# Turning round the column order of a decoder step's main products: moving columns read and sums written from last to first

## The chip, the cores and the metric

The kernel runs on one core of one Trainium2 chip. The metric is the device time of one execution in microseconds, lower being better; the runs shown are three executions of the kernel as it was. The profile is one execution taken by the hardware profiler. It names the engines PE (TensorE, matrix products), PEld (TensorE's loading of weights), DVE (VectorE), ACT (ScalarE), POOL (GpSimd) and SP (SyncE, which issues DMAs). L488 is line 488 of the kernel.

## The reference

The program computes one layer of a decoder for a prompt of 256 tokens and for 8 samples of 4 tokens each, which share all weights. Cut to what matters here:

```
h = rms_norm(x, g_mix)
proj = h @ w_in                       # conv, q, k, v, memory q, three gates
y_conv = silu(layer_norm(conv(...))) @ w_conv_out
y_sb   = stick_breaking(...) @ w_sb_out
y_mem  = memory_attend(...) @ w_mem_out
merged = g0 * y_conv + g1 * y_sb + g2 * y_mem
x = x + merged @ w_o
x = x + square(relu(rms_norm(x, g_mlp) @ w_up)) @ w_down
```

D_MODEL is 2048, the inner width of the last pair is 8192, all values are fp32. Besides the two outputs the program returns new keys, values, convolution states and memory keys and values.

## The kernel before

All activations stand transposed: a tile has 128 features on the partitions and the T = 288 tokens (256 of the prompt, then 32 of the samples) as columns. A weight matrix is cut into blocks of 128 x 128. Eight such blocks under each other, 512 KB, make a slab of `wall`, and the program walks through 504 slabs in one fixed order: w_kv, w_in, the branch projections between the gates, w_o, then four rounds of w_up and w_down.

Each slab is loaded by a DMA from SP into a buffer of pool `wr` (4 buffers). ScalarE rounds it into a high part of type fp32r in pool `wh` (L305), and VectorE takes the difference as a low part in pool `wl` (L316); each has 4 buffers. Activations are split in the same way, into `a.h` and `a.l`. One product then needs three matmuls for each block of 128 x 128: high weights with the high activations, high weights with the low ones, low weights with the high ones. `products` makes this list for a slab, 24 matmuls, and gives it to `chunk` in parts of six. `chunk` issues the matmuls (L488): the weights `w` are the stationary operand, 128 columns, and the activations `a` are the moving operand, 288 columns. All matmuls of one output tile add into the same bank of PSUM, `ps`, whose first 288 columns are used. `main_tile` takes two slabs (16 blocks of features) for one output tile of 128 features and then hands the bank to an evacuation on VectorE. `conv_products` calls `chunk` as well, for the first four tiles. The products of the prompt's memory tokens, in `mem_products` (L541, 512 moving columns), the attention's small products and the column sums in `total` (L443 and L444) do not go through `chunk`.

Where the operands lie in their tiles is fixed by a few constants:

```
APART = 320
AHEAD, HOME = 4, 36
PAD = 64
SHIFT = 5
```

Activations of pool `a` start at column 4 of a tile of 320 columns (`Acts`). The hidden activations of the last part live in `homes`, three to a buffer of pool `k4` from column 36 on, 320 columns apart, and one to a buffer of pool `s` from column 36 on. The weight slabs start at column 5 of their tile, apart from the first sixteen. The tiles of pool `t`, which `total` reads, and `ones_r` start at column 0.

The order of instructions on each engine is fixed by a planner (`Order`) when the program is built: jobs ask for an engine, a duration and buffers, and the one that can start first is taken, ties by rank. TensorE's instructions thus run in one planned order, and waits between engines are semaphores.

Of the kernel before, what the change touches and what calls it, by code (L numbers as in the profile page):

```python
# [183 lines left out]
def tile_decoder_step(ctx: ExitStack, tc: tile.TileContext, xT, memT, wall, cvec, kmat, ptab,  # L184
                      kpool, vpool, mkc, mvc, hist,
                      yT, oK, oV, oCp, oCs, oMK, oMV):
    nc = tc.nc
# [297 lines left out]

    def chunk(ps, todo, first, last):
        for i, (w, a) in enumerate(todo):
            nc.tensor.matmul(ps, w, a, start=(first and i == 0), stop=(last and i == len(todo) - 1))  # L488

    slab_no = [0]  # L490
    FULL = [k * P for k in range(8)]
# [2 lines left out]
    def products(ps, uses, acts, first=True, last=True, n=T):  # L494

        s = slab_no[0] - 1
        sl = slabs[s]
        high = [(sl.h, c, a, x) for c, a in zip(uses, acts) for x in (0, 1)]
        low = [(sl.l, c, a, 0) for c, a in zip(uses, acts)]
        todo = high + low  # L500
        for i in range(0, len(todo), STEP):
            part = todo[i:i + STEP]
            yield pe(len(part) * MM, *sl.split, *{a.flag for _, _, a, _ in part})
            if i == 0 and first:
                start_slab(s)
            chunk(ps, [(w[:, c:c + P], a.l if x else a.h) for w, c, a, x in part],
                  first and i == 0, last and i + STEP >= len(todo))
# [42 lines left out]
    def conv_products(evacs):  # L550
# [8 lines left out]
        for k2, o in turns:  # L559
            s = s0 + k2  # L560
            sl = slabs[s]
            if len(ps) <= o:
                yield pe(0.0, pm=1)
                ps.append(bank("pm")[:, :T])
            todo = []
            for i in range(2):
                w = slice(i * 512 + o * P, i * 512 + (o + 1) * P)
                todo += [(sl.h, w, "h", 2 * k2 + i), (sl.h, w, "l", 2 * k2 + i)]
            for i in range(2):
                todo.append((sl.l, slice(i * 512 + o * P, i * 512 + (o + 1) * P), "h", 2 * k2 + i))  # L570
            yield pe(6 * MM, *sl.split, hx_in[2 * k2], hx_in[2 * k2 + 1])
            if o == 0:
                start_slab(s)
            chunk(ps[o], [(w[:, c], getattr(hx[k], x)) for w, c, x, k in todo], k2 == 0, k2 == KT // 2 - 1)
            if k2 == KT // 2 - 1:
                add(evacs[o](ps[o]), 1.0 + 0.01 * o)
            if o == 3:
                give("w")
# [1042 lines left out]
```

## Time and profile before

| | |
|---|---|
| median of three runs | 1634.39 us |
| lowest, highest | 1634.28, 1634.63 us |
| span of the profiled execution, first to last instruction | 1632.5 us |
| matmuls | 12786, as many weight loads |
| matmuls of L488 | 11712 |
| HBM read | 297.05 MB, 186 GB/s over the span |
| granted TensorE clock | 1.000 |

The page gives busy time for each engine, the chain of work that ended last, and groups of instructions by line, with the busy time, the mean length of one, and the idle time before them. The length of a matmul is from its start to the modelled end of its results, so two matmuls that follow each other overlap; the distance between their starts is shorter than the length of one. That distance is read from a piece of the chain, or from a window, by dividing its length by the number of matmuls in it. The names on the two sides of the arrow are pools: `pm<-k,wl` is a matmul that writes a bank of pool pm and reads activations in a buffer of pool k4 and low weights.

### The profile page before, as it was taken

To read this page: it belongs to the slowest core of one execution; us is meant where nothing else is said; L and a number is where in the kernel's file an instruction comes from. 1 tells how busy PE (TensorE), PEld (TensorE's weight loads), DVE (VectorE), ACT (ScalarE), POOL (GpSimd) and SP (SyncE) were. 2 spreads that over 40 slices of the span, in tenths; PEclk is the share of its full clock that TensorE was granted. 3 is DMA by queue.
4 is the path that set the end of the run, shared out by engine and by line. 5 is a ranking of instruction groups with operands and counts; after the bars stand their busy time and mean duration, and the time that the engine had idled before them with its cause. 6 is when DMAs were issued, how large, how long until landed. Compare 5 with 4: busy or idle time off the path is not lost.

```text
span 1632.5 us, 30962 instructions
## 1 busy us (share of the span) xinstructions
PE 1627.7 (100%) x12786; PEld 1610.3 (99%) x12786; DVE 992.1 (61%) x1471; ACT 739.3 (45%) x1070; POOL 139.1 (9%) x104
## 2 busy tenths in 40 slices
PE   9999999999999999999999999999999999999999
PEld 7999999999999999999999999999999999999999
DVE  8889888877677655565555544455445554455443
ACT  8746766644444534444443333333333333333332
POOL 0020000000000000001222200121001210022100
PEclk9999999999999999999999999999999999999999
DMA  9787465777755555546655555555555555555563
GB/s 339 217 186 251 153 209 189 248 257 252 254 166 169 163 179 167 174 153 212 191 176 168 169 168 168 169 169 174 165 173 170 168 170 169 168 168 168 180 194 99
DMA packets 107103, 305.39 MB, mean 187 GB/s; under 512 B 19922, under 2 KB 29522, under 8 KB 106962
## 3 DMA queue, kind: packets, MB, share of 16 engines
q1 hardware_dynamic: 106818, 303.39, 58.2%
q8 instruction: 100, 1.64, 0.4%
q14 instruction: 41, 0.34, 0.1%
q10 hardware_dynamic: 144, 0.02, 0.0%
HBM read 297.05 MB, written 6.32 MB: 186 GB/s over the span
## 4 chain that ended last, share of the span: by engine, by line
PE 99%; DMA 0%; SPq 0%; ACT 0%; DVE 0%; issue 0%
PE pm L488 93%; PE pm L541 3%; PE pa L488 1%; PE pl L1017 1%; PE pl L1190 0%; PE pa L854 0%; PE pa L855 0%; PE pa L853 0%; DMA wr<-in_wall 0%; PE pl L1033 0%; PE pa L827 0%; PE pa L1144 0%; PE pa L908 0%; PE pa L1141 0%; PE pa L1143 0%; PE pa L1107 0%
## 5 line engine op out<-in xcount | busy, mean ns | idle before, releaser
L305 ACT CAST wh<-wr 128x1024 fp32r<-128x1024 f32 (+1 forms) x520 | 530.3, 1022 | 648.1 <-PE pm L488 597.0
L488 PE MATMUL pm<-a,wh 128*128 128x288 f32 x5184 | 739.1, 293 | 0.0
L316 DVE TENSOR_TENSOR wl<-wr,wh 128x1024 fp32r<-128x1024 f32 (+1 forms) x520 | 617.2, 1190 | 195.2 <-ACT wh L305 190.5
L488 PEld LDWEIGHTS pm<-a,wh 128*128 128x128 f32 x5184 | 696.7, 188 | 1.3 <-issue 1.2
L488 PE MATMUL pm<-a,wl 128*128 128x288 f32 x2592 | 397.0, 292 | 0.0
L488 PEld LDWEIGHTS pm<-a,wl 128*128 128x128 f32 x2592 | 358.4, 188 | 0.0
L488 PE MATMUL pm<-k,wh 128*128 128x288 f32 x2160 | 306.7, 292 | 0.0
L488 PEld LDWEIGHTS pm<-k,wh 128*128 128x128 f32 x2160 | 290.2, 188 | 0.0
L488 PE MATMUL pm<-k,wl 128*128 128x288 f32 x1120 | 171.6, 292 | 0.0
L488 PEld LDWEIGHTS pm<-k,wl 128*128 128x128 f32 x1120 | 155.1, 188 | 0.0
L1346 POOL TENSOR_TENSOR t<-t 128x288 f32<-128x288 f32 x64 | 96.7, 1511 | 599.5 <-DVE t L1343 599.5
L1360 DVE TENSOR_TENSOR a<-a,pm 128x288 f32<-128x288 f32 x64 | 29.0, 454 | 122.4 <-PE pm L488 122.4
L1343 DVE SCALAR_TENSOR_TENSOR t<-pm,rx 128x288 f32<-128x288 f32 x64 | 29.2, 457 | 90.4 <-PE pm L488 90.4
L1349 ACT CAST k<-t 128x288 fp32r<-128x288 f32 x56 | 24.1, 433 | 115.6 <-POOL t L1346 115.6
L1262 DVE TENSOR_TENSOR t<-pm,rx 128x288 f32<-128x288 f32 x48 | 22.0, 458 | 71.5 <-PE pm L488 71.5
L488 PE MATMUL pm<-s,wh 128*128 128x288 f32 x400 | 65.1, 292 | 0.0
L719 DVE SCALAR_TENSOR_TENSOR a<-a,cv,a 128x256 f32<-128x256 f32 x120 | 57.5, 480 | 1.4
L1332 POOL TENSOR_TENSOR t<-t,t 128x288 f32<-128x288 f32 x15 | 21.6, 1441 | 419.3 <-ACT t L1329 419.3
L488 PEld LDWEIGHTS pm<-s,wh 128*128 128x128 f32 x400 | 56.6, 188 | 0.0
L1351 DVE TENSOR_TENSOR k<-t,k 128x288 fp32r<-128x288 f32 x52 | 23.8, 458 | 51.1 <-ACT k L1349 51.1
L541 PE MATMUL pm<-wh,a 128*128 128x512 f32 x128 | 34.6, 391 | 0.2 <-ACT wh L305 0.2
L488 PE MATMUL pm<-s,wl 128*128 128x288 f32 x160 | 33.8, 292 | 0.0
(212 smaller groups left out, 784.4 us busy)
## 6 DMA issues: line engine op xcount, KB each, us to landing
wr<-in_wall SPq DMA_DIRECT2D x488, 512.0 KB, 3.6
wr<-in_wall SPq DMA_DIRECT2D x32, 256.0 KB, 4.8
k<-in_kpool SPq DMA_DIRECT2D x32, 256.0 KB, 5.9
k<-in_vpool SPq DMA_DIRECT2D x32, 256.0 KB, 5.8
k<-in_mkc SPq DMA_DIRECT2D x8, 512.0 KB, 10.2
k<-in_mvc SPq DMA_DIRECT2D x8, 512.0 KB, 6.5
t<-in_xT SPq DMA_DIRECT2D x16, 144.0 KB, 3.7
out_yT<-a SPq DMA_DIRECT2D x16, 144.0 KB, 1.9
```

The source lines that it names most:

```text
L305: nc.scalar.copy(sl.h[:, c], sl.raw[:, c])
L316: nc.vector.tensor_sub(sl.l[:, c], sl.raw[:, c], sl.h[:, c].bitcast(F32))
L488: nc.tensor.matmul(ps, w, a, start=(first and i == 0), stop=(last and i == len(todo) - 1))
L541: nc.tensor.matmul(ps[m], y[:, m * P:(m + 1) * P], z[:, w], start=(k == 0 and j < 2), stop=(k == KT - 1 and j in (4, 5)))
L719: nc.vector.scalar_tensor_tensor(c[:, :NP], up[:, k:k + NP], w, c[:, :NP], op0=ALU.mult, op1=ALU.add)
L1262: nc.vector.tensor_mul(g, ps, rx)
L1332: nc.gpsimd.tensor_add(sq_sum[0], sq_sum[0], res[0])
L1343: nc.vector.scalar_tensor_tensor(r, ps, 0.0, r2, op0=ALU.max, op1=ALU.mult)
L1346: nc.gpsimd.tensor_mul(r, r, r)
L1349: nc.scalar.copy(a.h, r)
L1351: nc.vector.tensor_sub(a.l, r, a.h.bitcast(F32))
L1360: nc.vector.tensor_add(x1[j], x1[j], ps)
```

## The change

One line of `chunk` is changed. The moving operand is given to the matmul as a view with its columns in reverse, and so is the output. Column 287 of the activations is read first and its sums are written to column 287 of the bank first; column 0 is last. Since both views are turned round, every sum lands where it did before. The stationary operand, the start and stop flags, the order of matmuls, all buffers, starts of tiles, engines and waits are as they were. Every engine has the same instructions in the same order.

```
 def chunk(ps, todo, first, last):
     for i, (w, a) in enumerate(todo):
-        nc.tensor.matmul(ps, w, a, start=(first and i == 0), stop=(last and i == len(todo) - 1))
+        nc.tensor.matmul(ps[:, ::-1], w, a[:, ::-1], start=(first and i == 0), stop=(last and i == len(todo) - 1))
```

## The prediction

> **What bounds the kernel now.** I read the page's table of busy time first, then the chain of waits, then what the TensorE itself waited for, and last how evenly it runs.
>
> ```profile
> span 1632.5 us, 30962 instructions
> PE 1627.7 (100%) x12786; PEld 1610.3 (99%) x12786; DVE 992.1 (61%) x1471; ACT 739.3 (45%) x1070; POOL 139.1 (9%) x104
> PEclk9999999999999999999999999999999999999999
> PE 99%; DMA 0%; SPq 0%; ACT 0%; DVE 0%; issue 0%
> PE pm L488 93%; PE pm L541 3%; PE pa L488 1%; PE pl L1017 1%; PE pl L1190 0%; PE pa L854 0%; PE pa L855 0%; PE pa L853 0%; DMA wr<-in_wall 0%; PE pl L1033 0%; PE pa L827 0%; PE pa L1144 0%; PE pa L908 0%; PE pa L1141 0%; PE pa L1143 0%; PE pa L1107 0%
> ```
>
> The chain that ends last is TensorE for 99% of the span, and line 488, the one line that the change edits, is 94% of it. Busy time alone would not prove this, since the ends of matmuls are modelled. The list of waits does: this is all that TensorE waited for other engines, and beside it the longest wait on the other side.
>
> ```profile
> PE pa L1409 <- POOL eps L234: 1.3, 1, 1.3
> PE pm L541 <- ACT wh L305: 0.2, 1, 0.2
> ACT wh L305 <- PE pm L488: 597.0, 341, 4.1
> ```
>
> TensorE lost 1.5 us to others in 1632.5 us. ScalarE, which casts the weights, waited 597.0 us for TensorE to free buffers. So the weights are always there early, and the time of this program is the number of matmuls times the pace at which TensorE takes them.
>
> That pace comes from the chain in order of time (start, length, how many), and does not depend on what else runs, as two windows show (PE, PEld, DVE, ACT and POOL busy, then the granted clock, the DMA share and GB/s).
>
> ```profile
> 17.79 31.28 PE pm L541 x138
> 541.70 297.18 PE pm L488 x2286
> 839.15 790.15 PE pm L488 x6078
> 600.00:700.00 100.00, 100.00 (x771) 100.00 (x770) 58.02 (x82) 42.75 (x55) 0.00 (x0) 1.00 0.54 168
> 1000.00:1200.00 200.00, 200.00 (x1541) 200.00 (x1540) 97.95 (x113) 72.56 (x80) 24.27 (x16) 1.00 0.54 169
> ```
>
> 790.15 us / 6078 = 130.0 ns from one matmul of 288 columns to the next, and 297.18 / 2286 = 130.0 ns too, over stretches that read their moving columns from three kinds of buffers. The windows give 129.7 ns with DVE 58% busy and 129.8 ns with DVE 49% busy. A pace this even is made inside each matmul, not by traffic of the other engines. The matmuls of 512 columns at line 541 take 31.28 / 138 = 226.7 ns. Two points give a line: (226.7 - 130.0) / (512 - 288) = 0.432 ns for a column, so 288 columns are 124.3 ns and 5.7 ns is left over for each matmul.
>
> **The change part by part.** It removes and adds no instruction and moves none; each engine has the same rows in the same order. The same sums land in the same columns of the same bank, because the moving columns and the output columns are both turned round. So VectorE reads what it read before and no wait changes. Only two address streams inside the matmul of line 488 run downwards: the moving read, from its tile's last column, and the accumulating write.
>
> How many matmuls that is, by group:
>
> ```profile
> L488 PE MATMUL pm<-a,wh 128*128 128x288 f32 x5184 | 739.1, 293 | 0.0
> L488 PE MATMUL pm<-a,wl 128*128 128x288 f32 x2592 | 397.0, 292 | 0.0
> L488 PE MATMUL pm<-k,wh 128*128 128x288 f32 x2160 | 306.7, 292 | 0.0
> L488 PE MATMUL pm<-k,wl 128*128 128x288 f32 x1120 | 171.6, 292 | 0.0
> L488 PE MATMUL pm<-s,wh 128*128 128x288 f32 x400 | 65.1, 292 | 0.0
> L488 PE MATMUL pm<-s,wl 128*128 128x288 f32 x160 | 33.8, 292 | 0.0
> L488 PE MATMUL pa<-a,wh 128*128 128x288 f32 x64 | 11.1, 295 | 0.0
> L488 PE MATMUL pa<-a,wl 128*128 128x288 f32 x32 | 6.8, 292 | 0.0
> ```
>
> Together 11,712. At 130.0 ns they are 1522.6 us of the 1632.5 us; the other 110 us (the 512-column products, the attention's small matmuls, start and tail) are not edited. So one nanosecond per matmul is worth 11.7 us, or 0.72%, and nothing hides it: TensorE is the chain. The profiled span lies 1.9 us under the median of the runs, 1634.39 us; I carry that as it is. The whole question is one number: what the 130.0 ns become.
>
> No row of this trace shows a matmul that reads or writes downwards. The only reversed operands are those of VectorE's scan at line 1204, another engine and an operation of its own. So I bound the cost from both sides.
>
> Below: the least that the fit leaves is the 124.3 ns of the columns, if turning the streams removed the whole 5.7 ns at the seam between two matmuls. 11,712 x 5.7 = 67 us, so 1567 us. The faster side cannot be excluded, since two streams are read side by side: the timeline has the weight load for the next matmul start with the present one.
>
> ```profile
> 1627.82 0.42 PE L488 MATMUL pm<-s,wh 128*128 128x288 f32 x2
> 1627.83 0.19 PEld L488 LDWEIGHTS pm<-s,wh 128*128 128x128 f32 x1
> ```
>
> The two starts are 0.01 us apart and the load takes 0.19 us, longer than the 0.130 us to the next matmul. Where a moving stream and a weight stream meet depends on where each starts and which way it runs.
>
> Above, in small: the matmuls of the same form (288 columns, fp32r, accumulated into a bank) whose tiles start at other columns. Lines 443 and 444 read a tile of pool t from its column 0 and weights from column 0 of ones_r, where line 488's start at columns 4 or 36 and its weights at column 5.
>
> ```profile
> L443 PE MATMUL pa<-t,ones_r x4: 294/295/297, 79.1 to 838.7; 128*128 128x288 f32 x4
> L444 PE MATMUL pa<-t,ones_r x4: 292/295/295, 79.3 to 838.9; 128*128 128x288 f32 x4
> L488 PE MATMUL pm<-a,wl x2592: 289/292/383, 54.6 to 1529.2; 128*128 128x288 f32 x200
> 838.88 0.13 PE pa L443
> 839.01 0.13 PE pa L444
> ```
>
> Median 295 ns against 292 ns for one, so +3 ns. In the chain the two occupy 838.88 to 839.15 us (the start of the next piece, quoted above), 0.27 us or 135 ns each against 130.0, so +5 ns at most. So where the streams start does matter, by some nanoseconds, and of the starts that this trace shows line 488's is the quickest. Turned round, the moving stream starts at column 291 (or 323, 643, 963 in the homes) and the sums at column 287. That is another start again, which I expect to fall between the present one and those rows: I take half of the +3 ns, +1.5 ns, and keep +5 ns (59 us, 1693 us) as the end.
>
> [...] What half pace looks like stands in the trace, for plain fp32 transposes:
>
> ```profile
> 153.59 0.27 PE L1107 MATMUL pa<-km,a 128*128 128x128 f32 x1
> 153.69 0.27 PE L1108 MATMUL pa<-km,a 128*128 128x128 f32 x1
> 153.80 0.27 PE L1109 MATMUL pa<-km,a 128*32 128x128 f32 x1
> 153.91 0.60 PE L908 MATMUL pa<-km,s 128*128 128x128 f32 x4
> ```
>
> They start 0.107 us apart for 128 columns, 0.83 ns a column against 0.43. This says that the slower pace exists, not that turning round brings it.
>
> [...]
>
> The sum for the likeliest case: 1634.4 + 11,712 x 1.5 ns = 1634.4 + 17.6 = 1652 us.
>
> **The rivals.**
>
> *Slightly faster.* The seam gets shorter: the place is the end of one 288-column stream and the start of the next, where the next weights are being read. It decides if the matmuls then start less than 129.7 ns apart. For it: 5.7 ns beyond the columns are there to be had, the other engines have room (DVE 61%, DMA 54% in the main stretch), and the casts are early, so that the gain would not turn into a wait. Against it: no matmul of this form in the trace is quicker than line 488's. Half of the 5.7 ns gives 1634.4 - 33 = 1601 us, all of it 1567 us.
>
> [...]
>
> [...]
>
> **How the numbers follow.** Slightly slower, 1638 to 1693 us, 0.36; slightly faster, 1567 to 1631 us, 0.30; nothing changes, 0.15; half pace or near it, 0.19. What a measurement can tell from no change here is about 0.2%, 3.3 us, or 0.28 ns per matmul. So faster 0.30, the same 0.15, slower 0.36 + 0.19 = 0.55. The prediction is 1652 us, the likeliest case; its own range is 1638 to 1693 us. The range over the cases, 1572 to 1693 us, leaves out half pace and the farthest end of the gain, 0.20 in all.
>
> **What would show it right or wrong.** Right: in the changed profile the long piece of line 488 in the chain lasts about 131.5 ns times its count, the mean of one is 293 to 295 ns instead of 292, with a, k and s alike, while line 541 stays at 226.7 ns and TensorE's waits stay under some 2 us. If k or s differ from a, the start column decides, not the direction. [...] Wrong altogether would be a changed wait: if TensorE starts to wait for wh or wl, or VectorE's reads of the sums take longer than in these rows, the change did more than turn two streams round.
>
> ```profile
> L1360 DVE TENSOR_TENSOR a<-a,pm 128x288 f32<-128x288 f32 x64 | 29.0, 454 | 122.4 <-PE pm L488 122.4
> L1343 DVE SCALAR_TENSOR_TENSOR t<-pm,rx 128x288 f32<-128x288 f32 x64 | 29.2, 457 | 90.4 <-PE pm L488 90.4
> ```

## The result and the profile after

The changed kernel takes 1672.54 us (median of 4 runs, 1672.34 to 1672.86) against 1634.51 us before (4 runs, 1634.28 to 1634.77): a ratio of 1.0232, 95% interval 1.0218 to 1.0247. It is 38.0 us slower. The profiled span grew by as much, from 1632.5 to 1670.7 us.

The page of the changed kernel, its busy times:

```profile
span 1670.7 us, 30962 instructions
PE 1666.1 (100%) x12786; PEld 1649.0 (99%) x12786; DVE 992.9 (59%) x1471; ACT 738.0 (44%) x1070; POOL 139.2 (8%) x104
```

The instructions are the same in number, and VectorE, ScalarE and GpSimd were busy for as long as before; only TensorE's time grew. What it waited for, in the list of waits of the same run (total, times, longest), is 1.3 us, against 1.5 us before:

```profile
PE pa L1409 <- POOL eps L234: 1.3, 1, 1.3
```

So no wait was added, and the casts still come early. The chain of waits of the changed kernel in order of time (start, length, how many) shows where the 38 us are:

```profile
17.93 31.28 PE pm L541 x138
551.98 304.80 PE pm L488 x2286
857.04 810.40 PE pm L488 x6078
```

810.40 us / 6078 = 133.3 ns from matmul to matmul where it was 130.0, and 304.80 / 2286 is 133.3 too. The products that were not edited, line 541, take the same 31.28 us. 3.33 ns on 11,712 matmuls are 39.0 us, 1 us more than the kernel lost, so nearly every one of them pays and nothing else does. The groups of the changed kernel, mean length of one in ns behind the comma, say that it does not depend on the buffer that is read (a, k or s):

```profile
L488 PE MATMUL pm<-a,wh 128*128 128x288 f32 x5184 | 756.2, 297 | 0.0
L488 PE MATMUL pm<-k,wh 128*128 128x288 f32 x2160 | 314.2, 297 | 0.0
L488 PE MATMUL pm<-s,wl 128*128 128x288 f32 x160 | 34.4, 297 | 0.0
L541 PE MATMUL pm<-wh,a 128*128 128x512 f32 x128 | 34.8, 394 | 0.0
L1360 DVE TENSOR_TENSOR a<-a,pm 128x288 f32<-128x288 f32 x64 | 29.2, 456 | 127.9 <-PE pm L488 127.9
```

The length of one grew by 5 ns (292 to 297) while the distance grew by 3.3: the length is from start to the modelled end of the results, and it is the distance that sets the time. VectorE reads the sums in 456 ns, as before (454).

### The profile page after: what moved, and what is told of

Read it like the earlier page. It is cut to its first block, busy times and chain, and to the rows that moved or that the text cites. A ratio compares the mean times of both kernels' runs of the same rounds, so it can differ in the third digit from the quotient of the medians.

```text
span 1670.7 us, 30962 instructions
## 1 busy us (share of the span) xinstructions
PE 1666.1 (100%) x12786; PEld 1649.0 (99%) x12786; DVE 992.9 (59%) x1471; ACT 738.0 (44%) x1070; POOL 139.2 (8%) x104
## 4 chain that ended last, share of the span: by engine, by line
PE 100%; POOL 0%; DVE 0%; issue 0%; POOLq 0%
PE pm L488 93%; PE pm L541 3%; PE pa L488 1%; PE pl L1017 1%; PE pl L1190 0%; PE pa L854 0%; PE pa L855 0%; PE pa L853 0%; PE pl L1033 0%; PE pa L1409 0%; PE pa L827 0%; PE pa L1144 0%; PE pa L908 0%; PE pa L1141 0%; PE pa L1143 0%; PE pa L1108 0%
## 5 line engine op out<-in xcount | busy, mean ns | idle before, releaser
L488 PE MATMUL pm<-a,wh 128*128 128x288 f32 x5184 | 756.2, 297 | 0.0
L488 PEld LDWEIGHTS pm<-a,wh 128*128 128x128 f32 x5184 | 712.0, 188 | 1.3 <-issue 1.2
L488 PE MATMUL pm<-a,wl 128*128 128x288 f32 x2592 | 405.8, 297 | 0.0
L488 PEld LDWEIGHTS pm<-a,wl 128*128 128x128 f32 x2592 | 365.4, 188 | 0.0
L488 PE MATMUL pm<-k,wh 128*128 128x288 f32 x2160 | 314.2, 297 | 0.0
L488 PEld LDWEIGHTS pm<-k,wh 128*128 128x128 f32 x2160 | 296.8, 188 | 0.0
L488 PE MATMUL pm<-k,wl 128*128 128x288 f32 x1120 | 175.5, 297 | 0.0
```

The costliest lines, as they stand in the source:

```text
L488: nc.tensor.matmul(ps[:, ::-1], w, a[:, ::-1], start=(first and i == 0), stop=(last and i == len(todo) - 1))
```

## The experiments

### Which of the two turned streams costs

The edit of the first is the read alone, that of the second the write alone.

```
-            nc.tensor.matmul(ps, w, a, ...)
+            nc.tensor.matmul(ps, w, a[:, ::-1], ...)        # e1_read
+            nc.tensor.matmul(ps[:, ::-1], w, a, ...)        # e2_write
```

> Only the moving read of line 488 runs from last to first; the sums are written from first to last, so each tile's token columns come out in reverse order (no instruction is left out). Theory R (the direction or start of the moving read, against the weight stream, makes the 3.3 ns per matmul): about 1672 us, 133.3 ns from matmul to matmul. Theory W (the accumulating write to PSUM does): 1634 us, 130.0 ns. Both in part: between them, with e1 and e2 adding up to 38 us.

> Only the sums of line 488 are written from last to first; the moving columns are read from first to last, so the token columns come out in reverse order (no instruction is left out). Theory R: 1634 us, 130.0 ns. Theory W: about 1672 us, 133.3 ns.

With the read alone the time is 1672.95 us, ratio 1.0233 (1.0215 to 1.0250). With the write alone it is 1634.90 us against 1634.91 us, ratio 1.000 (0.999 to 1.001). The longest piece of the chain, first of the kernel that turns the read:

```profile
857.53 810.40 PE pm L488 x6078
```

and of the kernel that turns the write:

```profile
839.60 790.15 PE pm L488 x6078
```

They are the lengths of the change and of the kernel before, to the hundredth of a microsecond. Theory R holds: the whole cost is the moving read, and sums written from last to first cost nothing that can be measured.

### Direction, or the place where the read starts

Turning the read round also moves its first column, from 4 to 291. Two kernels move the activations by one column in their tiles, one in reverse and one forward.

```
-AHEAD, HOME = 4, 36
+AHEAD, HOME = 5, 37        # e3_both_next, with the change
+AHEAD, HOME = 3, 35        # e4_fwd_prev, without the change
```

> The change as it is, with the activations one column further on in their tiles (AHEAD 5, HOME 37), so that the first moving column read is column 292 or 324, again 4 beyond a multiple of 32 as before the change. Theory S (not the direction but the first column's place against the weights' decides): back to about 1634 us. Theory D (the direction decides): 1672 us as the change.

> The kernel before, read and written from first to last, with the activations one column further back (AHEAD 3, HOME 35), so that the first moving column read is 3 beyond a multiple of 32 as in the change. Theory S: slower by up to 38 us, 1640 to 1672 us. Theory D: 1634 us.

In reverse and one column on, the time is 1698.84 us, ratio 1.0390 (1.0373 to 1.0408), 26 us more than the change. Forward and one column back it is 1653.70 us, ratio 1.0114 (1.0097 to 1.0131). The longest piece, first e3, then e4:

```profile
870.14 823.91 PE pm L488 x6078
```

```profile
848.90 800.28 PE pm L488 x6078
```

135.6 and 131.7 ns a matmul. Neither theory came out as written. Theory S was right that the start alone costs much, forward too, but the start that should have restored the old time made it worse; theory D was wrong that the start does not count. The forward kernel is slower by half as much as the change is without any reverse read, so place and direction had to be taken apart over many starts. The two kernels could not do it alone, also because both measure the place of the first column by multiples of 32, and the probe below repeats after 64 columns and not after 32.

### A table of paces

The probe leaves the layer out. Blocks of 48 matmuls run in the order of line 488, a list of 24 twice over, each block on a line of its own with its own starts. Cut to what sets the operands:

```
todo = [(WH, k, t[k]) for k in range(8) for t in (ah, al)] + [(WL, k, ah[k]) for k in range(8)]
...
        x, y = wt[:, w + k * P:w + (k + 1) * P], a[:, m:m + N]
        mm(out, ..., y[:, ::-1] if rd else y, ...)
```

> Not the decoder: a probe that leaves the whole layer out and runs blocks of 48 matmuls in the order of line 488 (eight weight blocks, high and low activations, 288 columns), each block on a line of its own, and reads the pace of each from the chain of waits. 32 lines read forward with the activations starting at columns 0 to 31 and weights at column 5, 32 lines the same in reverse, then 32 and 32 with activations at column 4 and weights at columns 0 to 31; last some with the sums written in reverse or from column 2, and some with 256 columns. Theory M (the moving stream and the weight stream meet in memory, and both starts and the direction set how often): the pace changes with both starts; forward 130.0 ns at start 4, 131.6 at 3, reverse 133.3 at 4, 135.5 at 5, and some reverse starts come down to about 130 ns. Theory D (reverse reading costs by itself): every reverse line lies at least 2 ns over the best forward line, whatever the start. Under both, writing in reverse changes nothing.

Eleven of its blocks in the chain of waits; the text names their starts, m for the activations' column and w for the weights'. Each probe was timed once. The first block of each, m 4 with w 5 at 165.4 to 193.1 ns, where the same starts later take 130.0, counts in none of the readings below. A block of 48 read to 0.01 us gives the pace to about 0.2 ns, so 131.0 ns here and the 131.1 ns of a whole kernel are the same pace. Of the blocks of 288 columns and full weights that stand in more than one probe, all but one (m 31, by 0.8 ns) agree to 0.2 ns.

```profile
35.13 6.32 PE pm L226 x48
41.45 6.24 PE pm L227 x48
47.70 6.42 PE pm L228 x48
66.84 6.29 PE pm L231 x48
246.67 6.40 PE pm L259 x48
253.07 6.50 PE pm L260 x48
272.56 6.29 PE pm L263 x48
452.90 6.40 PE pm L291 x48
655.50 6.30 PE pm L323 x48
857.25 6.25 PE pm L355 x48
863.50 6.41 PE pm L356 x48
```

Lines 226, 227 and 228 are forward, m 3, 4 and 5 with w 5: 131.7, 130.0 and 133.8 ns, the first two the paces of e4 and of the kernel before. Lines 259 and 260 are in reverse, m 4 and 5: 133.3 and 135.4 ns, the paces of the change and of e3. So the probe shows what the kernel does. Line 263 is in reverse with m 8: 131.0 ns. Line 231 is forward with m 8: 131.0 ns too. Line 323 is in reverse with m 4 again, and only the weights one column back, w 4: 131.2 ns. Line 291 is forward at these same starts, m 4 and w 4, and there it is the forward read that takes 133.3 ns. Lines 355 and 356 write the sums in reverse, with a forward and a reverse read: 130.2 and 133.5 ns, the write again without effect. Over all starts tried in this run with 288 columns, forward went from 130.0 to 139.6 ns and reverse from 131.0 to 139.6 ns. Both theories fell in their sharp form: the reverse read's best is only 1 ns over the forward read's, not 2, but it is not 130.0 either.

> The same probe (the layer is left out), with other starts, each block of 48 matmuls on its own line: activations at columns 32 to 63 with weights at 5, weights at 32 to 63 with activations at 4, forward and in reverse; both starts moved together; 128, 192 and 384 columns; and weight blocks of 96, 64 and 32 columns in place of 128. In the first probe the best forward block took 130.0 ns a matmul and the best reverse block 131.1 ns. Theory M (only meetings of the two streams cost, and the start can undo what the direction does): some of the new reverse starts come to 130.0 ns or less. Theory B (both: the direction has a floor of its own, the start the rest): no reverse block under 131.1 ns, while forward blocks reach 130.0 ns again. [...]

In the second probe, from the same view:

```profile
34.20 6.25 PE pm L226 x48
213.26 6.21 PE pm L254 x48
219.47 6.25 PE pm L255 x48
225.72 6.24 PE pm L256 x48
447.89 6.40 PE pm L291 x48
454.29 6.41 PE pm L292 x48
727.96 6.40 PE pm L335 x48
734.35 6.40 PE pm L336 x48
956.65 6.30 PE pm L371 x48
962.95 6.29 PE pm L372 x48
1043.75 6.40 PE pm L385 x48
1050.15 6.29 PE pm L386 x48
1119.99 6.24 PE pm L397 x48
1126.22 6.30 PE pm L398 x48
```

Lines 255 and 256 are forward with m 4 and 68, lines 335 and 336 the same in reverse: 64 columns further on (256 bytes) the pace is the same, 130 and 133.3 ns. Thirty-two columns further on it is not: m 36 takes 132.9 ns forward (line 227) and 131.7 in reverse (line 337). Line 254 is forward with m 63: 129.4 ns, the first start under 130. No reverse block came under 131.0 ns, as theory B said, though reverse was tried at 136 pairs of starts and forward, in all three probes, at 376. At these starts narrow weight blocks do not make the forward read quicker: with 32 columns of weights (lines 397 and 398) forward stays at 130.0 ns, and reverse is at 131.2. But they also show that the weight stream has a hand in it: with 96 columns (385 and 386), at the same starts as the change, it is forward that takes 133.3 ns and reverse that takes 131.0.

Two more readings of the same tables bear on the cause. First, which direction is quicker turns over with the starts. With both starts moved together, one column apart, m 0 and w 1 take 133.3 ns forward and 131.2 in reverse (lines 291 and 371), m 8 and w 9 133.5 and 131.0 (lines 292 and 372), while m 4 and w 5 take 130.0 and 133.3. Over the 136 pairs of starts that were tried both ways, reverse was slower by more than 0.3 ns at 66, quicker by as much at 50, and slower by 0.7 ns on average.

Second, the paces go by groups of four columns, 16 bytes. With w 5 and m from 0 to 63, the mean forward is 132.8, 135.6, 134.0 and 130.9 ns for m 0, 1, 2 and 3 columns beyond a multiple of four, and in reverse 132.1, 134.4, 135.0 and 136.4. Within a group single starts still differ by several ns. Of these 64 forward starts only nine take 130.2 ns or less, m 4 among them, and some 40 take 133.3 ns or more. So line 488 had one of the quickest starts before the change, and the 133.3 ns of the change are an ordinary pace for either direction.

The first column alone is not the cause. Counted in the 64 columns after which the pace repeated, the change's first column, 291, stands at 35, and a forward block with m 35 (line 226) takes 130.2 ns. That column 4 in pool a and column 36 in pools k4 and s behave alike in the kernel fits this count if the pools lie one behind another in the order in which they are opened: the 11 buffers of pool t between them, 288 columns each, are 49.5 times 64 columns. No trace gives the addresses.

> The probe (the layer is left out). First repeats: forward 130.0 ns at start 4, 129.3 ns at start 63, reverse 133.3 ns at 4 and 131.1 ns at 8. Then with weight blocks of 32 columns, 128 to 512 moving columns forward and in reverse: if the direction's 1.1 ns belongs to each matmul, the difference is the same for all widths; if it belongs to each column, it grows to 2 ns at 512. Last, forward blocks with activations at columns 3, 7 to 63 and weights at 0 to 15, to see whether starts under 130.0 ns exist beside 129.3 ns at 63 and 5.

In the third probe, of the same view, forward and in reverse by turns:

```profile
67.18 6.24 PE pm L233 x48
73.42 6.30 PE pm L234 x48
79.72 7.04 PE pm L235 x48
86.77 7.04 PE pm L236 x48
179.02 7.22 PE pm L247 x48
186.24 7.05 PE pm L248 x48
225.50 9.60 PE pm L253 x48
235.10 9.91 PE pm L254 x48
393.94 6.21 PE pm L277 x48
```

With 32 columns of weights, lines 233 and 234 (288 moving columns) differ by 1.2 ns, lines 235 and 236 (320 columns) not at all. With 128 columns of weights, reverse is 3.5 ns quicker at 320 columns (247 and 248) and 6.5 ns slower at 448 (253 and 254). So the direction's cost is neither a fixed sum for each matmul nor one for each column: both alternatives of the expectation fell, and reading downwards is not slow as such. Line 277 is forward with m 7 and w 4: 129.4 ns. The same pace came at m 7 with w 1, 7, 10 and 13, and at m 15 with w 6, 9, 12 and 15.

### Back in the kernel

Two kernels with the change as it is, one start moved in each, and one kernel without the change at a start from the third probe.

```
-AHEAD, HOME = 4, 36
+AHEAD, HOME = 8, 40        # e5_rev_start8, with the change
-SHIFT = 5
+SHIFT = 4                  # e6_rev_shift4, with the change
-AHEAD, HOME = 4, 36
-SHIFT = 5
+AHEAD, HOME = 7, 39        # e7_fwd_7_4, without the change
+SHIFT = 4
```

> The change as it is (whole layer), with the activations at columns 8 and 40 in place of 4 and 36, four columns on. In the probe reverse blocks went at 131.15 ns with activations at 8 and 133.3 ns at 4. Theory B (1.1 ns for the direction, 2.2 ns for where this reverse stream starts against the weights): 11,712 x 1.1 ns over before, so about 1648 us. If the start in the probe does not carry over to the kernel: 1672 us or more.

> The change as it is (whole layer), with the weight slabs starting at column 4 in place of 5 and the activations where they were. In the probe reverse blocks with weights at 4 went at 131.1 ns. Theory B: about 1648 us; nothing of the moving stream or of the sums is touched, so a gain here is the weight stream's. If only the moving stream counts: 1672 us.

> The kernel before (whole layer, read and written from first to last) with the activations at columns 7 and 39 in place of 4 and 36 and the weight slabs at column 4 in place of 5. In the probe such blocks went at 129.3 ns against 130.0 ns. If starts alone set the pace beside the direction and carry over: 11,712 x 0.7 ns under before, about 1627 us. If the kernel's mix of buffers breaks it: 1634 us or more.

With the activations four columns on, the changed kernel takes 1647.27 us, ratio 1.0075 (1.0057 to 1.0093). With the weights one column back it takes 1647.47 us, ratio 1.0077 (1.0059 to 1.0096). The longest pieces of e5 and of e6, in this order, agree:

```profile
845.80 796.91 PE pm L488 x6078
```

```profile
845.57 796.91 PE pm L488 x6078
```

Both are 131.1 ns. So 25 of the 38 us go away by moving either stream while the read stays in reverse, and moving the weights alone is enough, though no moving column and no sum has another address then. 12.5 us stay against the kernel before, but that kernel has other starts. The forward kernels with the starts of e5 and e6 were not run. By the probe's forward blocks at these starts (m 8: 131.0 ns; w 4: 133.3 ns) an estimate for them is 1647 and 1673 us, so that the reverse read would cost nothing in e5 and gain some 25 us in e6.

The forward kernel with the new starts takes 1626.72 us against 1634.90 us, ratio 0.9950 (0.9936 to 0.9963). Its longest piece:

```profile
835.29 786.10 PE pm L488 x6078
```

129.3 ns a matmul, as in the probe, for all kinds of buffers. It is the version that beats both kernels, the one before by 0.5%.

## Why the prediction was wrong

**What bounds the kernel: right.** Nothing but the pace of line 488 counts. TensorE's waits for others stayed under 2.3 us in every kernel, line 541 kept its pace in the changed one, and 11.7 us per nanosecond held within 1.2 us in every kernel that was run: 3.33, 5.55, 1.7, 1.1 and -0.7 ns a matmul gave 38, 64, 19, 12.5 and -8 us.

**The sign: right, with luck in it.** The forecast was slower because the stream starts elsewhere. That the starts of both streams count is shown by e3 to e7, and that all buffers would show the same was right too. But the new first column by itself does not do it (forward at m 35, 130.2 ns); it is the reverse order together with both starts. The sign hung on the layout: at other starts, m 4 with w 4 among them, the same change would go the other way by the probe. What spoke for slower, and stood in the prediction, is that line 488's start was the quickest in the trace.

**The size: wrong, and this is the step.** The prediction bounded the new start by lines 443 and 444, expected it "to fall between the present one and those rows", and took half of their +3 ns, +1.5 ns, 17.6 us. It measured +3.33 ns, 38.0 us, more than twice that. Two things failed in it. The +3 ns came from the length of one matmul, which is not the distance: in the changed kernel the length grew by 5 ns and the distance by 3.3. And halving assumed that the pace changes gently with the start. The table shows that it does not: one column further on is 1.7 ns less from m 3 to 4 and 3.8 ns more from m 4 to 5, and the order by groups of four is too rough, and differs too much between the directions, to place one start between two others. The end of +5 ns was no firmer. It came from two matmuls read to 0.01 us, and in the trace of the changed kernel, which leaves lines 443 and 444 as they were, the two take 0.26 us up to the next piece at 551.98, so 130 ns each where the prediction read 135:

```profile
551.72 0.13 PE pa L443
551.85 0.13 PE pa L444
```

With a pace that jumps, the middle carries no more evidence than the ends.

**Where the forecast put the cost: half right.** It had one number for the two streams that run downwards, the read and the write. The write alone costs nothing that can be measured, 1634.90 us and a ratio of 1.000 (e2); the read alone costs all of it, 1672.95 us (e1), 3.3 ns a matmul at this start. No run shows half pace, to which the forecast gave 0.19: the reverse read takes 0.46 ns a column in the change (133.3 / 288) and 0.47 in e3 (135.6 / 288), the slowest kernel that was run. The 0.83 ns a column of the transposes was no sign of it: in the probes matmuls of 128 columns on the fp32r tiles take 110.6 ns with 128 columns of weights (second probe, line 298), 0.86 ns a column, and 60.0 ns with 32 (third probe, line 227).

**The rivals.** "Nothing changes", to which the forecast gave 0.15, did not come: the reverse read from m 4 is slower, 133.3 ns against 130.0. "Slightly faster" named the meeting of the two streams as its place, and starts with less are there (e7), but the turned read at these starts is not one of them. Its 5.7 ns for the seam were not a measure of one: they came from two points at different starts, and the blocks with 32 columns of weights, 60.0 ns at 128 moving columns and 231.9 at 512 (third probe, lines 227 and 243), leave 2.7 ns by the same working, less than one step of a start can move. That "no matmul of this form in the trace is quicker" was true and said nothing of starts which the trace does not have.

**What is settled and what is open.** Settled: the 3.3 ns are in the moving read; 2.2 of them go away when either the activations or the weights move by a few columns, so they belong to how this reverse stream lies against the weights. Reading downwards has no fixed price: at the starts where these 2.2 ns are gone, the probe's forward blocks take as long or longer (m 8: 131.0 ns both ways; w 4: 133.3 forward, 131.2 in reverse). Open: why no reverse block of 288 columns in the probes was under 131.0 ns, while forward blocks reached 129.4; forward was tried at more starts, and 320 columns show no such gap. Open too is what makes the paces: that the two streams collide in memory is an inference from the fact that both starts count; no counter in the trace shows it.

## What to carry to other kernels

When TensorE is the whole chain, read its pace from a long piece of the chain divided by its count, and treat the start columns of both operands as parameters to be measured: in the kernels here they are worth from -0.5% to +1.1% forward, and up to +3.9% in reverse. A short probe with one block per line gave the time of the three full kernels that followed it to within 1 us, which reasoning from neighbouring rows did not. A view that turns the direction of an operand also changes its first address, so test one with the other held. And compare with the average start, not only with the one you have: a layout that happens to be among the quickest makes most changes of address look like a cost.

## What was not expected of the hardware

- Moving only the weights by 4 bytes changed the time of the changed kernel from 1672.5 to 1647.5 us, though TensorE's loads of them take the same 188 ns and overlap the matmuls.
- The paces of 288 columns came most often in a few steps that return again and again, 129.3, 130.0, 131.1, 131.7, 133.3 and 135.5 ns, and were the same 64 columns further on where that was tried (activations at 4 and 68, weights at 5 and 69).
- A reverse read can be the quicker one with the same starts: 146.9 ns against 150.4 at 320 columns, and 131.2 against 133.3 at 288 (m 4, w 4).
